# One core, a hybrid encoder block: token sums of x from a second copy, Strassen sums over twelve rounds, and matmuls of ones at the start

## The chip, the core and the metric

The kernel runs on one core of a Trainium2 chip. Its time is the device time of one execution in microseconds (us). A profile of one execution shows what each engine did: TensorE (PE, with its weight loads PEld), VectorE (DVE), ScalarE (ACT), GpSimd (POOL) and SyncE (SP), which issues most loads. Each engine works through its own instructions in a fixed order and waits for others by semaphores.

## The reference, cut to what matters

The block takes x (512 tokens of 2048 features, float32). Its first part is a normalisation by token and a product with a wide weight:

```python
def rms_norm(x, g):
    y = x32 * lax.rsqrt(jnp.mean(x32 * x32, axis=-1, keepdims=True) + EPS)
    return (y * g).astype(x.dtype)
a = rms_norm(h, attn_norm_g[i])
z = a @ w_in[i]          # q, k, v, and the two halves of a gated MLP
```

After it come differential attention with a relative-position bias, a spatial gate, an output product, a SwiGLU network, a gated per-layer input and a last normalisation. The change touches only the first normalisation and the first products.

## The kernel before, in words

All arrays are float32. A large product is made of three matmuls with a split operand: the high half is a cast to float32r (ScalarE, line 132, `whi`, or with a scale line 136), the low half is the value less that cast (VectorE, line 133, `wlo`, or line 137). A product is high by high, high by low and low by high. Each matmul is 128 by 128 by 512 columns.

x lies features by tokens (`xT`): 16 tiles of 128 features by 512 tokens. `load_x` (line 470) loads a tile on SyncE's queue and splits it, scaled by the norm's gain of the feature. The factor 1/rms of the token is applied to the products later.

The first stage (lines 507 to 554) makes three blocks of z. Blocks 0 and 1 are made together in eight rounds: a round loads four weight slabs of 128 by 256 (`load_w4`, line 510; in the first round as four loads and two splits, later as two loads and one split), loads x tiles two rounds' worth ahead, and does 24 matmuls (line 524, `products`). Block 2 follows in four rounds of the same size, 24 matmuls each; so there are 288 matmuls. Their results are stored by GpSimd's queue (line 530).

Beside its matmuls each of the eight rounds makes the Strassen sums of one pair of x tiles (`sums`, line 480): two scaled copies on ScalarE (lines 485, 486), four scaled sums on VectorE (line 493), and a split of the four (lines 132, 133). They are the stationary operand `op4` of the next stage, the stream over `w_vg` (`stream`, line 208, matmuls on line 316), which makes seven products instead of eight. `sums` also squares both x tiles on ScalarE (lines 425, 429) and GpSimd adds the squares (line 430). Early in the stream four small matmuls by ones (line 439) turn the added squares into sums by token, and `rsqrt` (line 445) makes the factors `rt`, which the stream's results need (line 570).

The order on each engine is laid down when the kernel is built, by a scheduler that takes instructions by priority as soon as their inputs are expected; `tc.high_priority` puts loads and splits of weights and of x ahead. On-chip memory is handed out in pools from the left and the right; when a pool is closed, tiles of a later pool may lie where its tiles lay, and then wait for their last use. The first stage's pools p0, p1, p2 lie at the right; the stream's w7x (four raw tiles, six halves) and b7x (four tiles `b12`, four `t1`) are opened at the left after those are closed.

Of the kernel before, what the change touches and what calls it, by code (L numbers as in the profile page):

```python
# [11 lines left out]
F32 = mybir.dt.float32  # L12
F32R = mybir.dt.float32r
AF = mybir.ActivationFunctionType
# [5 lines left out]
P = 128  # L20
D = 2048
T = 512
KT = D // P
# [8 lines left out]
CK = 4  # L32
# [3 lines left out]
RAWS = 4  # L36
PRIO = 80
FIRST = 4
XB = 12
KP = KT // 2  # L40
TAB = 3 * P
BIAS_W = 5 * P
# [31 lines left out]


@with_exitstack
def block_kernel(ctx: ExitStack, tc: tile.TileContext, out, xT, pT, w_in, w_vg, w_out, w13, w2,
                 w_up, w_gate, gains, fgain, subg, lam_v, rel_bias, onehot, lng, lnb, wsT, bsp):
    nc = tc.nc
    const = ctx.enter_context(tc.tile_pool(name="const", bufs=1))  # L80
    sm = ctx.enter_context(tc.tile_pool(name="sm", bufs=4))
    dr = ctx.enter_context(tc.tile_pool(name="dr", bufs=1, space=DRAM))
    pt = ctx.enter_context(tc.tile_pool(name="pt", bufs=2, space=PSUM))

# [4 lines left out]
    ident = const.tile([P, P], F32, name="ident")  # L89
    make_identity(nc, ident)  # L90
    ones = const.tile([P, P], F32, name="ones")
    nc.vector.memset(ones, 1.0)
    mhalf = const.tile([P, 4], F32, name="mhalf")
    nc.vector.memset(mhalf, -0.5)
    gain = const.tile([P, 2, KT], F32, name="gain")
    nc.scalar.dma_start(out=gain, in_=gains)
    ngain = const.tile([P, KT], F32, name="ngain")
    nc.vector.tensor_scalar(out=ngain, in0=gain[:, 0], scalar1=-1.0, scalar2=None, op0=ALU.mult)

# [345 lines left out]
    def rsqrt(ss, n, count, r=None):  # L445
        v = sm.tile([P, 4], F32, name="v")
        nc.vector.tensor_scalar(out=v[:, :n], in0=ss, scalar1=1.0 / count, scalar2=EPS,
                                op0=ALU.mult, op1=ALU.add)
        if r is None:
            r = sm.tile([P, 4], F32, name="r")  # L450
        nc.gpsimd.tensor_tensor(r[:, :n], v[:, :n], mhalf[:, :n], op=ALU.pow)  # L451
        return r
# [4 lines left out]
    ca = cap.__enter__()  # L457


    xop, xs, rt = [], [], []  # L460
    zqk = dr.tile([3, P, 2, T], F32, name="zqk")
    zg = dr.tile([2, 2, P, 2, T], F32, name="zg")
    with pool("osm", bufs=1) as osm:
        pcp, pap, pbp = (pool(n, side="right", bufs=1) for n in ("p0", "p1", "p2"))
        pc, pa, pb = pcp.__enter__(), pap.__enter__(), pbp.__enter__()
        pp = ctx.enter_context(ppp := ExitStack()).enter_context(
            pool("ppx", bufs=1, space=PSUM))
        rms = Rms(D, pc.tile([P, T], F32, name="acc"))

        def load_x(n):  # L470
            for k in range(len(xop), min(n, KT)):
                xt = pb.tile([P, T], F32, name="xt", bufs=XB)
                o = op_tile(opa)
                with tc.high_priority(PRIO):
                    nc.sync.dma_start(out=xt, in_=xT[:, k])
                    split((o[:, 0], o[:, 1]), xt, gain[:, 0, k:k + 1])
                xop.append(o)
                xs.append(xt)

        def sums(c):  # L480
            (g0, g1), n0 = (gain[:, 0, 2 * c + e:2 * c + e + 1] for e in range(2)), \
                ngain[:, 2 * c:2 * c + 1]
            x11, x21, x12, x22 = (xs[2 * c + e][:, n:n + 256] for e in range(2) for n in (0, 256))
            a = pa.tile([P, 2, 256], F32, name="a2")
            nc.scalar.activation(a[:, 0], x22, AF.Copy, scale=g1)
            nc.scalar.activation(a[:, 1], x11, AF.Copy, scale=g0)
            for e in range(2):
                rms.add(xs[2 * c + e], pa)
            t = pa.tile([P, 4, 256], F32, name="t4")
            for o, x, y, v, f in ((0, x21, a[:, 0], g0, ALU.add), (1, x11, t[:, 0], n0, ALU.add),  # L490
                                  (2, x12, t[:, 1], g1, ALU.subtract),
                                  (3, x21, a[:, 1], n0, ALU.add)):
                nc.vector.scalar_tensor_tensor(out=t[:, o], in0=x, scalar=v, in1=y, op0=ALU.mult,
                                               op1=f)
            o = osm.tile([P, 4, 2, 256], F32R, name="op4", bufs=KP)
            split((o[:, :, 0], o[:, :, 1]), t)
            return o

        def stationary(c, o):
            def at(i, x, s):  # L500
                if 0 < i < 5:
                    return o[:, i - 1, x, s * P:(s + 1) * P]
                n = s + (2 if i == 6 else 0)
                return xop[2 * c + (i > 0)][:, x, n * P:(n + 1) * P]
            return at

        load_x(1)
        ps = [pp.tile([P, 2, T], F32, name="c", bufs=3) for _ in range(3)]

        def load_w4(src):  # L510
            raw = pb.tile([P, CK, 256], F32, name="raw", bufs=3)
            hi = pa.tile([P, CK, 256], F32R, name="whi", bufs=2)
            lo = pa.tile([P, CK, 256], F32R, name="wlo", bufs=2)
            with tc.high_priority(PRIO):
                for u, v in src:
                    for i, w in u:
                        nc.sync.dma_start(out=raw[:, i], in_=w)
                    split((hi[:, v], lo[:, v]), raw[:, v])
            return hi, lo

        def products(ps, hi, lo, n, k):
            for m in range(2):
                for i, (a, b) in enumerate(((hi, 0), (hi, 1), (lo, 0))):
                    nc.tensor.matmul(ps[:, m], lhsT=a[:, n, m * P:(m + 1) * P], rhs=xop[k][:, b],  # L524
                                     start=k == 0 and i == 0, stop=k == KT - 1 and i == 2)

        def store(j, n):
            t = ca.tile([P, 2, T], F32, name=n)
            nc.vector.tensor_copy(t, ps[j])
            nc.gpsimd.dma_start(out=zqk[j], in_=t)  # L530

        sop = []
        for c in range(KP):
            u = [[(slice(2 * j + n, 2 * j + n + 1) if c == 0 else slice(2 * j, 2 * j + 2),
                   w_in[4 * j, :, 2 * c + n:2 * c + n + (1 if c == 0 else 2)]) for j in range(2)]
                 for n in range(2 if c == 0 else 1)]
            hi, lo = load_w4([(u[n], slice(n, 4, 2)) for n in range(2)] if c == 0
                             else [(u[0], slice(0, 4))])
            load_x(2 * c + 3)
            for k in range(2):  # L540
                for j in range(2):
                    products(ps[j], hi, lo, 2 * j + k, 2 * c + k)
            sop.append(stationary(c, sums(c)))
        for k0 in range(0, KT, CK):
            hi, lo = load_w4([([(slice(0, CK), w_in[1, :, k0:k0 + CK])], slice(0, CK))])
            if k0 == 0:
                store(0, "c21")
                store(1, "c12")
            for j in range(CK):
                products(ps[2], hi, lo, j, k0 + j)  # L550
        store(2, "c21")
        pbp.__exit__(None, None, None)
        pap.__exit__(None, None, None)
        pcp.__exit__(None, None, None)


        cbp = pool("cb", side="right", bufs=1)
        cb = cbp.__enter__()
        z = {}

        def result(g, n):
            z[n] = (ca if n in ("c12", "c21") else cb).tile([P, 2, T], F32, name=n)
            return z[n]

        def finish_z(g, n, t, later, s=None, acc=None):
            u, f = int(n[1]) - 1, int(n[2]) - 1
            for s in range(2):
                nc.scalar.activation(t[:, s], (t if acc is None else acc)[:, s],
                                     AF.Copy if g else AF.Gelu_apprx_tanh,
                                     scale=rt[0][:, 2 * u + s:2 * u + s + 1])  # L570
            if not g:
                nc.gpsimd.dma_start(out=zg[u, f], in_=t)

        with pool("w7x", bufs=1) as w7, pool("b7x", bufs=1) as b7:
            stream(w7, w7, b7, b7, pp, [Phase(
                w_vg, [(g, 0, KP // 2) for g in range(2)], lambda g, k: sop[k],
                combine(result, finish_z), at={2: [(lambda: rt.append(rms.token()), ())]})])
        ppp.close()
    rt = rt[0]
    wpp = pool("wpa", bufs=2)  # L580
    rp = wp = wpp.__enter__()
    pscp = pool("psc", bufs=1, space=PSUM)
# [37 lines left out]
    def prelude():  # L620
        diag = hp.tile([P, 4, P], F32, name="diag", tag="aT")
        for t in range(4):
            nc.vector.tensor_scalar(out=diag[:, t], in0=ident, scalar1=rt[:, t:t + 1],
                                    scalar2=None, op0=ALU.mult)
        ps = pt.tile([P, T], F32, name="pt")
        nc.tensor.matmul(ps, lhsT=ones, rhs=diag.rearrange("p t q -> p (t q)"), start=True,
# [189 lines left out]
    sop = []  # L816
# [394 lines left out]
```

## Time and profile before

| | us |
|---|---|
| median of 3 runs | 2188.73 |
| lowest, highest run | 2186.42, 2191.08 |
| profiled execution, its own time | 2185.85 |
| span from its first to its last instruction | 2183.7 |
| TensorE busy | 2130.8 (98%) |
| VectorE busy | 1640.0 (75%) |
| ScalarE busy | 1026.9 (47%) |
| GpSimd busy | 249.1 (11%) |

The mean granted clock of TensorE is 0.994 of 2.4 GHz. Times in rows count from the span's start. A matmul's time in a row is from its start to its modelled end, and matmuls overlap; how far starts lie apart tells their pace.

### The profile page before, as it was taken

Reading aid. Unit: us, or ns where it says so; the run is one execution under the profiler, and the core shown is the slowest. Engines: PE = TensorE matmul, PEld = TensorE weight load, DVE = VectorE, ACT = ScalarE, POOL = GpSimd, SP = SyncE. Lnnn points to the kernel's source line nnn. Section 1 sums busy time; section 2 is a strip of 40 time slices with the busy share of each in tenths; the row PEclk is TensorE's granted clock in tenths of the full one; section 3 lists DMA queues with packets and bytes.
Section 4 is the critical chain, followed back from the end, with each engine's and each line's share of the span. In section 5 each row is a group of like instructions: output and inputs, shape, how many; then the busy total and the mean of one; then the engine's idle time right before and its main releaser. Section 6 shows DMA issues by size and latency. Waiting matters only on the chain. (4 is left out here: it accounts for less than half of the span.)

```text
span 2183.7 us, 25457 instructions
## 1 busy us (share of the span) xinstructions
PE 2130.8 (98%) x9514; PEld 1745.2 (80%) x9514; DVE 1640.0 (75%) x1762; ACT 1026.9 (47%) x1295; POOL 249.1 (11%) x378
## 2 busy tenths in 40 slices
PE   7999999999999899999999999999999999999997
PEld 5788777878887688888888888888778888888885
DVE  8677565455535787798788788778788877789896
ACT  6354323355434454554555455455443333346555
POOL 4000300001221000000000000003312202100000
PEclk9999999999999999999999999999999999999999
DMA  5443532223445435534544553557967837536535
GB/s 174 164 147 105 180 108 68 87 78 108 143 138 185 120 121 159 191 121 141 183 151 128 176 173 129 160 186 219 317 230 224 269 116 233 179 111 215 192 105 179
DMA packets 112346, 350.24 MB, mean 160 GB/s; under 512 B 12976, under 2 KB 14512, under 8 KB 112224
## 3 DMA queue, kind: packets, MB, share of 16 engines
q1 hardware_dynamic: 67904, 233.86, 34.6%
q0 software_dynamic: 41056, 107.16, 14.4%
q10 hardware_dynamic: 3264, 7.62, 0.9%
q8 instruction: 74, 1.21, 0.2%
q14 instruction: 48, 0.39, 0.1%
HBM read 286.46 MB, written 62.13 MB: 160 GB/s over the span
## 5 line engine op out<-in xcount | busy, mean ns | idle before, releaser
L316 PE MATMUL c<-whi,op 128*128 128x512 f32 x4592 | 1422.6, 391 | 8.7 <-ACT op L198 5.7
L316 PEld LDWEIGHTS c<-whi,op 128*128 128x128 f32 x4592 | 858.2, 188 | 188.4 <-ACT op L198 6.4
L316 PE MATMUL c<-wlo,op 128*128 128x512 f32 x2296 | 895.6, 390 | 7.2 <-DVE wlo L133 7.1
L132 ACT CAST whi<-raw 128x1024 fp32r<-128x1024 f32 (+1 forms) x331 | 347.0, 1050 | 489.7 <-PE c L316 290.8
L133 DVE TENSOR_TENSOR wlo<-raw,whi 128x1024 fp32r<-128x1024 f32 (+1 forms) x331 | 403.3, 1221 | 216.8 <-ACT whi L132 211.9
L316 PEld LDWEIGHTS c<-wlo,op 128*128 128x128 f32 x2296 | 431.3, 188 | 101.5 <-DVE wlo L133 11.2
L132 ACT CAST whi<-t 128x1024 fp32r<-128x1024 f32 x246 | 259.1, 1053 | 314.1 <-PE c L316 283.9
L168 PE MATMUL ps<-op,whi 128*128 128x512 f32 x1088 | 349.1, 400 | 0.0
L133 DVE TENSOR_TENSOR wlo<-t,whi 128x1024 fp32r<-128x1024 f32 x246 | 299.8, 1220 | 34.0 <-ACT whi L132 32.3
L239 DVE TENSOR_TENSOR t<-raw,t 128x1024 f32<-128x1024 f32 x164 | 200.5, 1222 | 78.4 <-DMA raw<-w 64.7
L168 PEld LDWEIGHTS ps<-op,whi 128*128 128x128 f32 x1088 | 201.3, 188 | 44.4 <-issue 3.6
L168 PE MATMUL ps<-op,wlo 128*128 128x512 f32 x544 | 213.4, 392 | 0.0
L395 POOL DMA_DIRECT2D gs<-o x88 | 47.3, 538 | 768.0 <-DVE o L133 718.1
L132 ACT CAST whi<-b 128x1024 fp32r<-128x1024 f32 x82 | 86.4, 1054 | 87.7 <-PE c L316 87.7
L133 DVE TENSOR_TENSOR wlo<-b,whi 128x1024 fp32r<-128x1024 f32 x82 | 100.1, 1221 | 33.1 <-ACT whi L132 32.8
L168 PEld LDWEIGHTS ps<-op,wlo 128*128 128x128 f32 x544 | 102.1, 188 | 21.6
L239 DVE TENSOR_TENSOR b<-raw,b 128x1024 f32<-128x1024 f32 x82 | 100.1, 1221 | 20.1 <-DMA raw<-w 18.0
L939 POOL DMA_DIRECT2D op<-gs x154 | 83.1, 540 | 253.2 <-PE c L316 238.9
L239 DVE TENSOR_TENSOR t<-b,raw 128x1024 f32<-128x1024 f32 x82 | 101.3, 1236 | 5.7 <-DMA b<-w_vg 2.3
L340 DVE TENSOR_TENSOR c<-c,c 128x1024 f32<-128x1024 f32 x63 | 76.9, 1221 | 14.0 <-PE c L316 14.0
L132 ACT CAST o<-t 128x512 fp32r<-128x512 f32 x88 | 49.1, 569 | 76.3 <-DMA gs<-o 48.1
L524 PE MATMUL c<-op,whi 128*128 128x512 f32 x192 | 61.9, 404 | 9.0 <-ACT whi L132 9.0
(173 smaller groups left out, 1230.8 us busy)
## 6 DMA issues: line engine op xcount, KB each, us to landing
raw<-w SPq DMA_DIRECT2D x198, 512.0 KB, 3.8
op<-gs POOLq DMA_DIRECT2D x154, 256.0 KB, 4.7
b<-w SPq DMA_DIRECT2D x66, 512.0 KB, 4.4
gs<-o POOLq DMA_DIRECT2D x66, 512.0 KB, 3.3
raw<-w_in SPq DMA_DIRECT2D x40, 512.0 KB, 3.6
raw<-w_out SPq DMA_DIRECT2D x32, 512.0 KB, 3.6
raw<-w_vg SPq DMA_DIRECT2D x24, 512.0 KB, 3.6
raw<-w_gate SPq DMA_DIRECT2D x24, 512.0 KB, 4.2
```

Source lines behind the costliest of these rows:

```text
L132: recent[:] = (nc.scalar.copy(out=hi, in_=src), nc.vector.tensor_tensor(out=lo, in0=src, in1=hi.bitcast(F32), op=ALU.subtract))
L133: nc.vector.tensor_tensor(out=lo, in0=src, in1=hi.bitcast(F32), op=ALU.subtract))
L168: nc.tensor.matmul(ps[:, m], lhsT=a[:, j, ms], rhs=op[k][:, b], start=k == 0 and i == 0, stop=k == nk - 1 and i == 2)
L239: nc.vector.tensor_tensor(o, x, y, op=ALU.subtract)
L316: product[:] = [nc.tensor.matmul(p, lhsT=f.op(g, k)(i, x, s), rhs=y[:, e], start=k == 0 and i in (0, 1, 5) and (x, y) == (0, whi), stop=k ...
L340: (eng or nc.vector).tensor_tensor(o, x, y, op=ALU.add)
L395: nc.gpsimd.dma_start(out=gs[j, :, n:n + m], in_=o[:, :m].bitcast(F32))
L524: nc.tensor.matmul(ps[:, m], lhsT=a[:, n, m * P:(m + 1) * P], rhs=xop[k][:, b], start=k == 0 and i == 0, stop=k == KT - 1 and i == 2)
L939: nc.gpsimd.dma_start(out=sop[p + e][:, i], in_=gs[k + e, :, i])
```

## The change

A second copy of x by tokens (`xn`, four blocks of 128 tokens by 2048) becomes an input. Four times, GpSimd's queue loads a block into one tile and ScalarE squares it and adds each row up in the same instruction; `rsqrt` on the four columns gives `rx`, which takes the place of `rt`. The squares by feature, GpSimd's additions and the four matmuls by ones in the stream go. The Strassen sums are made in rounds 2 to 5 and 7 to 10 of the twelve, the squares in rounds 1, 3, 5 and 7. x has sixteen tiles instead of twelve. The first round's weights are split in four quarters, each behind its own load. A small copy on ScalarE and ten 128x128 matmuls of ones by ones come right after the constants. A tile of 64 bytes is put in the left-hand memory.

```diff
-XB = 12
+    ctx.enter_context(tc.tile_pool(name="padl", bufs=1)).tile([P, 16], F32, name="padl")
     nc.scalar.dma_start(out=gain, in_=gains)
+    nc.scalar.copy(out=const.tile([P, 4], F32, name="first"), in_=mhalf)
+    ps = pt.tile([P, T], F32, name="pt")
+    for _ in range(10):
+        nc.tensor.matmul(ps[:, :P], lhsT=ones, rhs=ones, start=True, stop=True)
...
-        rms = Rms(D, pc.tile([P, T], F32, name="acc"))
+        ssx = pc.tile([P, 4], F32, name="ssx")
+        def squares_x(t):
+            x = pc.tile([P, D], F32, name="xn", bufs=1)
+            nc.gpsimd.dma_start(out=x, in_=xn[t])
+            nc.scalar.activation(x, x, AF.Square, accum_out=ssx[:, t:t + 1])
...
-                xt = pb.tile([P, T], F32, name="xt", bufs=XB)
+                xt = pb.tile([P, T], F32, name="xt", bufs=KT)
...
-            for e in range(2):
-                rms.add(xs[2 * c + e], pa)
...
+        def step(n):
+            for c in {2: (0,), 3: (1,), 4: (2,), 5: (3,), 7: (4,), 8: (5,), 9: (6,), 10: (7,)}.get(n, ()):
+                sop.append(stationary(c, sums(c)))
+            if n in (1, 3, 5, 7):
+                squares_x(n // 2)
         for c in range(KP):
-            hi, lo = load_w4([(u[n], slice(n, 4, 2)) for n in range(2)] if c == 0
-                             else [(u[0], slice(0, 4))])
+            if c == 0:
+                hi, lo = load_w4([([(slice(2 * j + n, 2 * j + n + 1), w_in[4 * j, :, n:n + 1])],
+                                   slice(2 * j + n, 2 * j + n + 1)) for n in range(2)
+                                  for j in range(2)])
+            else:
+                hi, lo = load_w4([([(slice(2 * j, 2 * j + 2), w_in[4 * j, :, 2 * c:2 * c + 2])
+                                    for j in range(2)], slice(0, 4))])
...
-            sop.append(stationary(c, sums(c)))
+            step(c)
         for k0 in range(0, KT, CK):
...
+            step(KP + k0 // CK)
+        rx = const.tile([P, 4], F32, name="rx")
+        rsqrt(ssx, 4, D, rx)
...
-                combine(result, finish_z), at={2: [(lambda: rt.append(rms.token()), ())]})])
+                combine(result, finish_z))])
```

## Rows read from the trace of the kernel before

**Rows 1.** Busy time by stretch: stretch, length, engines, granted clock, DMA share, GB/s.

```profile
8.23:68.00 59.77, 52.46 (x207) 40.35 (x208) 57.31 (x65) 39.86 (x63) 23.83 (x16) 0.97 0.45 146
10.00:15.00 5.00, 5.00 (x19) 3.94 (x18) 5.00 (x8) 5.00 (x9) 2.05 (x1) 1.00 1.02 370
43.38:46.44 3.06, 3.06 (x7) 2.44 (x8) 3.03 (x3) 1.30 (x3) 2.68 (x2) 0.52 0.56 170
```

**Rows 2.** TensorE's waits, 0 to 250 us: total, times, longest.

```profile
PE c L524 <- ACT whi L132: 9.0, 2, 8.2
PE c L524 <- DVE wlo L133: 6.6, 5, 3.3
PE c L316 <- ACT whi L132: 0.7, 2, 0.5
```

**Rows 3.** Instructions grouped, 0 to 87 us: busy, mean ns, idle before.

```profile
L430 POOL TENSOR_TENSOR acc<-acc,sq 128x512 f32<-128x512 f32 x15 | 23.5, 1566 | 28.7 <-ACT sq L429 28.1
...
L137 DVE SCALAR_TENSOR_TENSOR op<-xt,gain,op 128x512 fp32r<-128x512 f32 x16 | 15.7, 1003 | 0.8 <-ACT op L136 0.8
...
L132 ACT CAST whi<-raw 128x1024 fp32r<-128x1024 f32 x13 | 13.4, 1044 | 5.9 <-PE c L524 5.7 <-ACT whi L132 0.2
...
L429 ACT ACTIVATE sq<-xt 128x512 f32<-128x512 f32 x15 | 8.9, 621 | 2.5 <-POOL acc L430 2.5
...
L493 DVE SCALAR_TENSOR_TENSOR t<-xt,gain,a 128x256 f32<-128x256 f32 x8 | 7.8, 969 | 0.1
L493 DVE SCALAR_TENSOR_TENSOR t<-xt,ngain,a 128x256 f32<-128x256 f32 x8 | 6.9, 864 | 0.0
L493 DVE SCALAR_TENSOR_TENSOR t<-xt,gain,t 128x256 f32<-128x256 f32 x8 | 5.7, 713 | 0.2
L493 DVE SCALAR_TENSOR_TENSOR t<-xt,ngain,t 128x256 f32<-128x256 f32 x8 | 4.8, 606 | 0.0
```

**Rows 4.** Lines 493 and 137 by themselves: ns shortest, median, longest.

```profile
L493 DVE SCALAR_TENSOR_TENSOR t<-xt,gain,a x8: 476/936/1527, 9.6 to 65.0; 128x256 f32<-128x256 f32 x8
...
L137 DVE SCALAR_TENSOR_TENSOR op<-xt,gain,op x16: 740/746/1780, 5.9 to 41.4; 128x512 fp32r<-128x512 f32 x16
```

**Rows 5.** TensorE in order of time: start, duration, instruction.

```profile
8.23 1.22 PE L524 MATMUL c<-op,whi 128*128 128x512 f32 x2 [8.23 <-ACT whi L132]
...
12.24 0.63 PE L524 MATMUL c<-op,whi 128*128 128x512 f32 x2
...
77.70 0.61 PE L524 MATMUL c<-op,whi 128*128 128x512 f32 x2
...
86.54 0.61 PE L316 MATMUL c<-whi,op 128*128 128x512 f32 x2
...
96.42 0.95 PE L439 MATMUL pt<-ones,acc 128*128 128x1 f32 x8
97.23 0.49 PE L316 MATMUL c<-wlo,op 128*128 128x512 f32 x1
```

**Rows 6.** All engines in order of time, the first 8 us.

```profile
0.83 0.17 DVE L92 MEMSET ones<- 128x128 f32 x1 [0.83 <-PEq L1201]
...
1.28 0.72 POOL L612 DMA_DIRECT2D sg<-subg  x1 [0.34 <-issue]
...
3.81 1.28 ACT L136 ACT_TABLE_LOAD   x1 [3.81 <-DMA xt<-xT]
...
7.58 1.12 ACT L132 CAST whi<-raw 128x512 fp32r<-128x512 f32 x2
```

**Rows 7.** TensorE's instructions grouped, whole span: busy, mean ns, idle before.

```profile
L758 PE MATMUL pt<-wb,z 128*128 128x128 f32 x64 | 8.6, 278 | 0.3 <-DVE mixed L762 0.3
```

**Rows 8.** SyncE's queue in order of time, about the turn to the stream.

```profile
65.44 1.95 SPq L229 DMA_DIRECT2D raw<-w_vg  x4
86.50 1.75 SPq L229 DMA_DIRECT2D b<-w_vg  x4
```

**Rows 9.** DMA issues, 0 to 260 us: KB each, median us to landing.

```profile
zqk<-c POOLq DMA_DIRECT2D x3, 512.0 KB, 8.3
```

More of the change, by code (lines that the diff above doesn't have):

```diff
@@ L76, in block_kernel @@
 @with_exitstack
-def block_kernel(ctx: ExitStack, tc: tile.TileContext, out, xT, pT, w_in, w_vg, w_out, w13, w2,
+def block_kernel(ctx: ExitStack, tc: tile.TileContext, out, xT, xn, pT, w_in, w_vg, w_out, w13, w2,
                  w_up, w_gate, gains, fgain, subg, lam_v, rel_bias, onehot, lng, lnb, wsT, bsp):
@@ L457, in block_kernel @@
     ca = cap.__enter__()
-    xop, xs, rt = [], [], []
+    xop, xs = [], []
     zqk = dr.tile([3, P, 2, T], F32, name="zqk")
@@ L532, in block_kernel @@
         sop = []
-        for c in range(KP):
-            u = [[(slice(2 * j + n, 2 * j + n + 1) if c == 0 else slice(2 * j, 2 * j + 2),
-                   w_in[4 * j, :, 2 * c + n:2 * c + n + (1 if c == 0 else 2)]) for j in range(2)]
-                 for n in range(2 if c == 0 else 1)]
-            hi, lo = load_w4([(u[n], slice(n, 4, 2)) for n in range(2)] if c == 0
-                             else [(u[0], slice(0, 4))])
+        def step(n):
[3 more added lines that the diff above has]
+                squares_x(n // 2)
+        for c in range(KP):
+            if c == 0:
[5 more added lines that the diff above has]
+                                    for j in range(2)], slice(0, 4))])
             load_x(2 * c + 3)
@@ L569, in finish_z @@
                                      AF.Copy if g else AF.Gelu_apprx_tanh,
-                                     scale=rt[0][:, 2 * u + s:2 * u + s + 1])
+                                     scale=rx[:, 2 * u + s:2 * u + s + 1])
             if not g:
@@ L576, in block_kernel @@
                 w_vg, [(g, 0, KP // 2) for g in range(2)], lambda g, k: sop[k],
-                combine(result, finish_z), at={2: [(lambda: rt.append(rms.token()), ())]})])
+                combine(result, finish_z))])
         ppp.close()
-    rt = rt[0]
     wpp = pool("wpa", bufs=2)
@@ L622, in prelude @@
         for t in range(4):
-            nc.vector.tensor_scalar(out=diag[:, t], in0=ident, scalar1=rt[:, t:t + 1],
+            nc.vector.tensor_scalar(out=diag[:, t], in0=ident, scalar1=rx[:, t:t + 1],
                                     scalar2=None, op0=ALU.mult)
@@ L1178 @@
         "xT": _tokens(a["x"][0]),
+        "xn": np.ascontiguousarray(a["x"][0].reshape(T // P, P, D)),
         "pT": _tokens(a["p"][0, 0]),
```

## The prediction

> **What bounds the kernel now.** TensorE is busy for 98% of the span, so only stretches in which it waits or runs at half rate can give time back. I read the table of stretches first, then TensorE's waits in the first 250 us, then the instructions of those stretches. From 8.23 to 68 us VectorE is busy for 57.3 of 59.8 us, more than TensorE (52.5), and GpSimd works for 23.8 us beside it [rows 1]. TensorE's waits there end with the two weight splits, ScalarE's high half and VectorE's low half: 9.0 us in two waits, of which 8.2 are the start, and 6.6 us in five [rows 2]. After that, up to 250 us, there is 0.7 us of waiting. So the place of the change is the only stage of the first 250 us with much to give.
>
> Why VectorE is late is in the grouped instructions. The 32 Strassen sums of x (L493) have means of 969, 864, 713 and 606 ns, the 16 low halves of x (L137) 1003 ns [rows 3]; but the shortest of a sum is 476 ns, the median of L137 746 ns, and the longest 1527 and 1780 ns [rows 4]. The long ones lie beside GpSimd's 15 additions of squares (L430, 1566 ns each). Without that neighbour the sums would take 32 x 0.476 = 15.2 us instead of 25.2, the low halves 11.9 instead of 15.7 (their minima and medians): 13.8 us of VectorE's 57 are lost to GpSimd.
>
> **How much lies in the stage.** Its matmuls start at 8.23 and the stream's first starts at 86.54, 78.31 us for 288 matmuls. Where nothing waits, 39 of them start between 77.70 and 86.54: 0.2267 us each [rows 5], so the 288 need 65.3 us and 13.0 us are lost after the start. Of these the first nine take 4.01 us (8.23 to 12.24) instead of 2.04: 2.0 us at half rate. After the wait of 3.3 us seven more take 3.06 us instead of 1.59, with a granted clock of 0.52, the 1.2 GHz level [rows 1]: 1.5 us. Waits after the start are 7.4 us; the rest, 2.1 us, is the tail of matmuls drawn longer than their spacing, and lies with the waits.
>
> **The change part by part.**
>
> *Token sums from a copy by tokens.* Sixteen squares of 128x512 on ScalarE (621 ns) and fifteen additions on GpSimd go. Four squares of 128x2048 come: by the squares' 621 ns for 512 columns and the cast's 1044 ns for 1024 [rows 3], 0.83 ns a column, so an estimate of 1.9 us each, 7.6 for 9.9 before. GpSimd's neighbour work and the 13.8 us go. The four small matmuls by ones at 96.42 go too: the next product starts at 97.23, so 0.8 us [rows 5].
>
> *Sums over twelve rounds.* A round has 24 matmuls, 5.44 us. VectorE's work in one, undisturbed: two low halves of x 1.49, the low half of the weights 1.22, four sums 1.9, their low half 1.22, in all 5.8 us by durations (somewhat less, since starts follow closer than durations); without sums 2.7. Before, all eight rounds have sums: 46 us against TensorE's 43.5, and 60 with GpSimd. Now five of the first eight do: 8 x 2.7 + 5 x 3.1 = 37 us. The other three go into rounds with one weight split, 1.22 + 3.1 = 4.3 us. VectorE is no longer the bound in any long run of rounds. ScalarE in rounds 3, 5 and 7 has two high halves of x (1.4), a cast of weights and one of sums (1.04 each), two scalings (1.0) and a square (1.9): 6.4 us, over 5.44, but 2.4 to 4.5 in the rounds between. So the 11.0 us of waits and lowered clock inside the stage should nearly all go; bounds 0 and 11.0.
>
> *Start.* Before, ScalarE begins its table load when x lands, at 3.81, and then splits three x tiles ahead of the weights' cast at 7.58 [rows 6]. Now a copy of a small tile takes the 1.28 us load before the data, and the first cast needs a quarter of the tile. The first split from 3.81 takes 0.7, a 128x256 operation of ScalarE 0.5: the earliest matmul is at 5.0, the latest at 8.2 as now. I take 5.6, since later loads share the queue: 2.6 us. Four quarter operations for two half ones cost two more starts on ScalarE, and on VectorE: 0.4 us, which I charge.
>
> *Matmuls of ones.* A matmul of 128x128 in float32 shows as two records: 64 for the 32 calls of L758, 8.6 us, 0.134 us each at the upper clock [rows 7]. Ten calls are 2.7 us at 2.4 GHz, 5.4 at 1.2. They can start when the ones are written, 1.00 [rows 6], and end between 3.7 and 6.4, so they hold the first product up by 0.8 us at most. Before, the rate rises after 4.0 us of work [rows 5]; about as much work now lies ahead of the first product. I credit the 2.0 us; bounds 0 and 2.0.
>
> *New cost: 4.2 MB of x again.* GpSimd has no work before the first of these loads; that it issues early what stands far down in the program is seen in L612's load at 1.28 [rows 6]. So the first 1.05 MB comes with the first weights. From 10 to 15 us the engines of the DMA are full, share 1.02 at 370 GB/s [rows 1]; at that rate 1.05 MB are 2.8 us. The first rounds need 1.05 MB each in 5.44 us, 193 GB/s, and the copy 96 GB/s more if it keeps two rounds apart: 289, under 370. So a delay at the start, none later: bounds 0 and 2.8, taken 2.0. By the Trainium skill's page "DMA: Bandwidth & Descriptors", section "Issuing engines are not separate DMA queues", loads from GpSimd and from SyncE run on the same 16 engines, so the second queue gives nothing but issue time; by it the sum would carry the full 2.8 for 2.0. No run of before has both queues loaded in this stage.
>
> *New wait.* Each square waits in ScalarE's queue for its load, and behind it stand casts of weights, for which TensorE waits. The next load waits for the square before, since there is one buffer. A round or two of distance covers it; for a first one placed early I charge 1.5 us, and 0.5 for rounds 3, 5 and 7. Bound 0 below; above, see the last rival.
>
> *Nothing.* The rsqrt on four values lies beside products. Sixteen x tiles instead of twelve take away a wait of the load queue. On GpSimd's queue the loads L612 and L614 and the three stores of products now stand behind loads of the copy; the first two are used after the stream, and the stores come after the last square's load.
>
> **The sum.** Off: 2.6 + 2.0 + 11.0 + 0.8 = 16.4 us. On: 0.4 + 2.0 + 1.5 + 0.5 = 4.4. Net 12.0 us. After the stage TensorE hardly waits, so the gain stays. The profiled execution took 2185.85 us (span 2183.7 and 2.15 around), the median of the timed ones 2188.73, 2.9 more. 12.0 off give 2173.9 against the first and 2176.7 against the median, which I predict.
>
> **The rivals.**
>
> *The start is starved.* If the copy is loaded as fast as its buffer comes free, 4.2 MB compete with the first five rounds, not one. At 370 GB/s that is 11.3 us of transfer; slack is 370 - 193 = 177 GB/s, so over the 27 us of five rounds 4.8 MB fit, and the loss is uneven delivery, say 4 to 6 us more: 2181.5. For: the share of 1.02. Against: the waits of TensorE end with splits, none with a load [rows 2]. Chance 0.15. The rule of the skill's page named above points this way.
>
> *The turn to the stream.* Twelve x tiles become sixteen and an 8 KB tile comes, while 2 KB of sums and two 2 KB squares go: the right-hand pools grow by 10 KB. The stream's first four raw tiles, which now load at 65.44 without a wait, may come to lie on them; its other four already wait for the last product, to 86.50 [rows 8]. If all wait, TensorE stands still for landing and split, some 5 us, and 1.5 at the lower clock: 2183.2. Against: x tiles are free when their sums are done, a round before the end. Chance 0.10.
>
> *ScalarE takes VectorE's place.* It has 6.4 us in every second round, and its small waits meet VectorE's. Then only start, clock and the four small matmuls remain, 5.4, less 4.4: 2187.7, within the 0.2% (4.4 us) that a measurement can tell. Against: 39.9 us of ScalarE in 59.8 [rows 1]. Chance 0.08.
>
> *Slower: squares hold ScalarE up.* If the order written out for ScalarE puts each square right behind the load's expected landing and the load is later than expected, all casts wait. ScalarE's own work in the first eight rounds is about 32 us (39.9 less three sums' share and some of the squares). With four waits of w, the stage ends at 5.6 + 32 + 4w + 21.8 (four rounds); that passes 86.54 at w = 6.8 us. Transfers of half that size from GpSimd's queue took 8.3 us from issue to landing [rows 9]. With w = 8.3 it ends at 92.6, later by 6.1, less 0.8: 2194.0. Against: in the program the squares stand two rounds, 10.9 us, apart. Chance 0.06.
>
> **How the numbers follow.** The forecast has the remaining 0.61, with its own range of 2172 to 2180. Low end: all 16.4 off and the lowest run, 2.3 under the median, 2170. High end: the first two rivals with an execution's spread, 2185; beyond it lie the last two cases. Faster by over 0.2% are the forecast, nearly all of the first two rivals: 0.84; within 0.2% 0.10; slower 0.06.
>
> **What would show it.** Right: ten matmuls of ones from about 1 us; the first product at 5 to 6.5, at full spacing; L493 near 0.48 us throughout; VectorE's share before 68 us well under its 96%; no granted clock below 1.00 in the stage; the stream's first product at 73 to 76. Wrong: TensorE waiting for ScalarE's casts behind L429's successor, a wait of the load queue at the turn, first products beyond 8 us, or a stage that ends early while the span does not shrink.

## The result, and the profile after

The changed kernel takes 2205.81 us (median of 5 runs, 2204.07 to 2208.5), the kernel before beside it 2187.07 (5 runs, 2185.71 to 2191.08): a ratio of 1.009, 95% interval 1.0079 to 1.0102. The forecast was 2176.7 us. The profiled execution took 2204.07 us with a span of 2202.0, 18.3 more than before.

One row splits that. The stream's first product comes at 80.76 us (86.54 before, [rows 5]), so 5.8 us are won up to there; from it to the end it is 2121.2 us for 2097.2, so 24.0 are lost in a stretch that the diff hardly touches.

TensorE of the changed kernel in order of time (start, duration, instruction, in brackets the wait before it):

```profile
1.05 3.93 PE L100 MATMUL pt<-ones 128*128 128x128 f32 x20 [1.05 <-DVE mhalf L94]
4.97 0.99 PE L531 MATMUL c<-op,whi 128*128 128x512 f32 x2
...
12.04 2.07 PE L531 MATMUL c<-op,whi 128*128 128x512 f32 x4 [5.04 <-ACT whi L136]
...
17.32 0.82 PE L531 MATMUL c<-op,whi 128*128 128x512 f32 x2
...
77.95 0.64 PE L531 MATMUL c<-op,whi 128*128 128x512 f32 x2
...
80.76 0.63 PE L320 MATMUL c<-whi,op 128*128 128x512 f32 x2
```

The first product starts at 4.97 instead of 8.23. Then TensorE stands still for 5.04 us, and runs at half rate after that: the 12 matmuls between 12.04 and 17.32 take 5.28 us, where 12 x 0.2267 are 2.72. At the end of the stage nothing waits, and still the 12 matmuls between 77.95 and 80.76 take 2.81 us, 0.234 each. In [rows 5] 39 of them took 8.84, 0.227 each.

The same kernel by stretches (stretch, length, busy time of PE, PEld, DVE, ACT, POOL with counts, granted clock, DMA share, GB/s):

```profile
2.00:10.00 8.00, 5.00 (x24) 3.83 (x22) 1.66 (x4) 2.14 (x6) 0.31 (x1) 1.00 0.90 291
...
8.23:68.00 59.77, 55.96 (x228) 44.87 (x229) 47.78 (x71) 42.22 (x59) 4.93 (x8) 0.94 0.72 247
...
12.00:14.00 2.00, 1.96 (x5) 1.58 (x6) 1.96 (x5) 2.00 (x2) 0.00 (x0) 0.50 0.93 323
14.00:16.00 2.00, 2.00 (x6) 1.55 (x5) 1.39 (x4) 2.00 (x6) 1.50 (x3) 0.50 1.09 368
...
700.00:1500.00 800.00, 793.06 (x3500) 644.91 (x3499) 647.24 (x664) 402.03 (x465) 42.25 (x76) 1.00 0.47 149
```

and the last stretch in the kernel before:

```profile
700.00:1500.00 800.00, 792.35 (x3560) 654.03 (x3559) 656.98 (x675) 407.61 (x470) 45.43 (x82) 1.00 0.48 154
```

VectorE has 47.78 us of work in the stage for 57.31 [rows 1]. The granted clock is 0.50, the 1.2 GHz level, behind the wait. In the 800 us far behind the stage TensorE is as busy as before at a granted clock of 1.00, and has done 60 matmuls fewer: 1.7%. So no wait and no clock explains the loss; each matmul takes longer.

VectorE and ScalarE of the changed kernel, grouped, 0 to 82 us (busy, mean ns, idle before):

```profile
L500 DVE SCALAR_TENSOR_TENSOR t<-xt,gain,t 128x256 f32<-128x256 f32 x8 | 3.9, 484 | 0.2
L500 DVE SCALAR_TENSOR_TENSOR t<-xt,gain,a 128x256 f32<-128x256 f32 x8 | 3.9, 481 | 0.3
...
L477 ACT ACTIVATE xn<-xn 128x2048 f32<-128x2048 f32 x4 | 7.6, 1908 | 1.5 <-DMA xn<-xn 1.5
```

The Strassen sums take 0.48 us each, as forecast, and the squares 1.91 each. TensorE's waits of over 0.15 us, 0 to 100 us (total, times, longest); the last line is of the stream:

```profile
PE c L531 <- ACT whi L136: 5.0, 1, 5.0
PE pt L100 <- DVE mhalf L94: 1.1, 1, 1.1
PE c L320 <- ACT whi L136: 0.7, 2, 0.5
```

So in the stage it waits for nothing after 12.04.

### The profile page after: what moved, and what is told of

It reads as the page before. It is cut to its first block, busy times and chain, and to the rows that moved or that the text cites. A ratio compares the mean times of both kernels' runs of the same rounds, so it can differ in the third digit from the quotient of the medians.

```text
span 2202.0 us, 25455 instructions
## 1 busy us (share of the span) xinstructions
PE 2161.0 (98%) x9526; PEld 1752.6 (80%) x9526; DVE 1628.9 (74%) x1764; ACT 1027.0 (47%) x1290; POOL 226.6 (10%) x367
## 4 chain that ended last, share of the span: by engine, by line
PE 91%; DMA 3%; DVE 3%; issue 2%; ACT 1%; POOL 0%; SPq 0%; DVEq 0%; POOLq 0%; ACTq 0%
PE c L320 67%; PE ps L172 16%; PE c L531 3%; DMA raw<-w 2%; DVE wlo L137 1%; PE c L302 1%; PE pt L384 1%; PE sc L709 1%; PE pt L740 1%; DVE t L243 0%; DMA xt<-xT 0%; ACT whi L136 0%; PE pt L776 0%; PE pt L844 0%; DMA bias<-dtab 0%
## 5 line engine op out<-in xcount | busy, mean ns | idle before, releaser
L320 PE MATMUL c<-whi,op 128*128 128x512 f32 x4592 | 1439.9, 395 | 8.5 <-ACT op L202 5.7
L320 PE MATMUL c<-wlo,op 128*128 128x512 f32 x2296 | 905.0, 394 | 4.8 <-DVE wlo L137 4.7
```

The lines of the kernel that those rows point to most:

```text
L320: product[:] = [nc.tensor.matmul(p, lhsT=f.op(g, k)(i, x, s), rhs=y[:, e], start=k == 0 and i in (0, 1, 5) and (x, y) == (0, whi), stop=k ...
```

## The experiments

Ratios are against the kernel before on the same chip (its medians there: 2185.73, 2185.47, 2185.83 and 2185.38), with 95% intervals. "Tail" is the time from the stream's first product to the end of the span in the profiled execution. It is one execution of each kernel, and those of one kernel can lie 10 us apart (e4: 2177.15 to 2187.44), so a tail that is some us longer is a sign, and the medians and intervals decide.

| run | median us | ratio | stream's first | tail |
|---|---|---|---|---|
| before | 2185.38 to 2187.07 | 1 | 86.54 | 2097.2 |
| changed | 2205.81 | 1.009 [1.0079, 1.0102] | 80.76 | 2121.2 |
| e3: before, left +128 bytes | 2208.91 | 1.0103 [1.0088, 1.0118] | 86.92 | 2122.6 |
| e8: before, both sides +128 | 2185.91 | 0.9999 [0.999, 1.0009] | 86.98 | 2097.1 |
| e11: before, left +64 | 2194.4 | 1.0042 [1.0027, 1.0058] | 87.28 | 2102.7 |
| e1: changed, left as before | 2187.06 | 1.0005 [0.9996, 1.0015] | 80.46 | 2105.5 |
| e2: e1, right as before too | 2185.2 | 1.0001 [0.9991, 1.0011] | 80.55 | 2102.0 |
| e4: e2, first copy held | 2183.92 | 0.9991 [0.9979, 1.0002] | 80.08 | 2101.1 |
| e5: e4, four ones | 2177.79 | 0.9966 [0.9954, 0.9978] | 78.20 | 2096.9 |
| e6: before, six ones | 2191.4 | 1.0021 [1.0012, 1.003] | 86.26 | 2105.5 |
| e12: before, 64 ones | 2204.87 | 1.0091 [1.0076, 1.0106] | 104.85 | 2097.0 |
| e13: before, 70 ones | 2212.84 | 1.0128 [1.0111, 1.0145] | 107.61 | 2102.3 |
| e7: e5, copy from round 4 | 2174.4 | 0.9946 [0.9933, 0.996] | 74.63 | 2096.9 |
| e10: e7, sums in eight rounds | 2174.66 | 0.9945 [0.9932, 0.9957] | 74.98 | 2097.7 |

**Theories.** First theory: the diff's small tiles shift whole memory regions, and a matmul's pace depends on how the addresses of its two operands stand to each other. By the addresses that the compiler gave, all split operands of the kernel before start at 128 past a multiple of 256 bytes. In the changed kernel those in the left-hand memory start at a multiple of 256, those at the right still at 128 past, the stage's weights at 96. The left side has moved by 128 bytes: 64 of the tile in the diff, 32 that ScalarE's small copy takes, and 32 because `rx` and the later `rt` no longer share one place. Rivals: the new order of the instructions makes the long stretch slower, or the loads of the copy do.

**e1, e3: the left side alone.** e1 puts the left-hand tiles of the changed kernel back to 128; e3 moves those of the kernel before, and changes nothing else.

```diff
# e1, from the changed kernel
-tile_pool(name="padl", bufs=1)).tile([P, 16], F32, name="padl")
+tile_pool(name="padl", bufs=1)).tile([P, 48], F32, name="padl")
# e3, from the kernel before
+ctx.enter_context(tc.tile_pool(name="padl", bufs=1)).tile([P, 32], F32, name="padl")
```

> The changed kernel with the left-hand pad tile at 192 bytes a partition instead of 64, so that the left-hand tiles lie a further 128 bytes up and are again congruent modulo 256 bytes with the right-hand ones. Theory (the pace of a matmul depends on whether its moving and its stationary operand start at the same address modulo 256 bytes): the 6216 matmuls of the later streams go back from 231 to 227 ns, some 27 us less, about 2179 us against 2187 of the kernel before (0.996); the first stage stays at 234 ns. Rival (the 18.7 us are waits or contention of the new order, and the pad is without effect): 2206, 1.009.

> The kernel before with nothing but a left-hand pad tile of 128 bytes a partition. Theory: its first stage and its later streams fall to 231 to 234 ns where the operands now differ by 128 modulo 256, the stream over w_vg and the products of w_in and w_out stay at 227; about 28 us more, 2215 (1.013). Rival (the loss is of the new order): as before, 2187, 1.000.

e1 wins 18.7 us of the 27 expected over the changed kernel, and an unused tile of 128 bytes alone makes the kernel before as slow as the changed one. The 800 us of e3, then of e1, by the same columns as above:

```profile
700.00:1500.00 800.00, 792.85 (x3494) 644.57 (x3493) 648.01 (x664) 400.97 (x462) 46.36 (x75) 0.99 0.48 150
```

```profile
700.00:1500.00 800.00, 788.73 (x3535) 649.13 (x3534) 651.30 (x672) 405.92 (x468) 45.10 (x81) 1.00 0.48 152
```

e3 has 66 matmuls fewer than the kernel before without any of the change's instructions; that is against both rivals. e1 gets 35 of the changed kernel's 60 back, not all.

**e8, e11: is it the address or the difference?** e8 shifts both sides by 128 bytes; e11 the left by 64.

```diff
# e8, from the kernel before
+ctx.enter_context(tc.tile_pool(name="padl", bufs=1)).tile([P, 32], F32, name="padl")
-tile_pool(name="pad", side="right", bufs=1)).tile([P, 24], F32, name="pad")
+tile_pool(name="pad", side="right", bufs=1)).tile([P, 56], F32, name="pad")
# e11, from the kernel before
+ctx.enter_context(tc.tile_pool(name="padl", bufs=1)).tile([P, 16], F32, name="padl")
```

> The kernel before with both pads 128 bytes larger, so that all tiles of both sides lie 128 bytes further in and are congruent with each other again. Theory (only the difference of the operands' addresses modulo 256 bytes counts): pace 227 ns and time as before, 2186 (1.000). Rival (each operand's own address counts): slower as with the left pad alone, 2209 (1.010).

> The kernel before with nothing but a left-hand pad tile of 64 bytes a partition, so that the operands of the first stage and of five eighths of the later streams differ by 64 bytes modulo 256. Theory: slow as with 128 bytes, 231 to 234 ns for a matmul, 2205 to 2212 us (1.010). Rival (only a difference of 128 counts, or the grain is 64 bytes): as before, 2186 (1.000).

With both sides shifted the time is that of before; so it is the difference that counts. 64 bytes cost 8.6 us, 128 cost 23: neither expectation for e11 had a step in between. Every matmul of the first stage, the streams and the products with w_in and w_out, matched with its operands' addresses, gives the start-to-start pace (of those under 300 ns whose next matmul has the same pair of addresses; the last two rows are of the first stage, the others of the streams):

| addresses modulo 256 bytes, moving and stationary operand | matmuls | mean ns | median ns |
|---|---|---|---|
| 0 and 0 (e8) | 6720 | 227.1 | 227 |
| 192 and 192 (e11) | 2548 | 227.5 | 227 |
| 192 and 128 (e11) | 3592 | 229.3 | 229 |
| 0 and 128 (e3) | 3594 | 232.7 | 232 |
| 0 and 0 (e3) | 2534 | 228.1 | 227 |
| 128 and 96 (e1, first stage) | 271 | 233.5 | 234 |
| 0 and 96 (changed, first stage) | 270 | 234.3 | 234 |

3594 x (232.7 - 227.1) = 20.1 us of e3's 23, and 3592 x (229.3 - 227.1) = 7.9 of e11's 8.6. In the kernel before the two addresses differ by 0, 256, 512 or 768 bytes modulo 1024, 2053 to 2199 matmuls of each, and the median is 227 ns for all four; so 256 is the grain. The loss does not grow with the distance: 32 apart (e1's first stage) costs as much as 96 or 128, 64 apart less than half. Why the hardware does this was not settled.

**e2: the right side too.** A tile of 56 floats beside the small tile of squares' sums puts the stage's weights back to 128 past.

```diff
         ssx = pc.tile([P, 4], F32, name="ssx")
+        pc.tile([P, 56], F32, name="padr")
```

> As the run before, and a 224-byte pad tile beside the tile of row sums on the right, so that the first stage's weights are congruent too. Theory: the first stage's 288 matmuls also go from 234 to 227 ns, 2 us more, about 2177 us (0.995). Rival (address without effect): 2206, 1.009.

Addresses now stand as before, yet e2 is level with the kernel before, not 2177. The stage's matmuls are back at 227 ns, but it still ends at 80.55: the first product comes 0.3 us later than in e1, at 5.34, and there are two waits for low halves, 1.0 us, that the changed kernel does not have. The tail is 2102.0, 4.8 longer than before. So the stage and the tail each hide another loss.

**e4: the copy's first load.** Its tile is first written by a small copy that needs the last quarter of the first weights, so the load can't start before them.

```diff
             x = pc.tile([P, D], F32, name="xn", bufs=1)
+            if t == 0:
+                nc.vector.tensor_copy(x[:, 0:1], last[0][:, 3, 0:1].bitcast(F32))
```

> The second run's kernel, with the first load of the copy by tokens held until VectorE has made the low half of the last quarter of the first weights (one extra 128x1 copy on VectorE). Theory (the first load of the copy takes half of the DMA engines from the first x tiles and weights, so that TensorE waits 5.0 us at 7 us and then runs at half rate): that wait falls under 1 us, the half rate does not come back, the stream's first product starts 5 to 7 us sooner, about 2171 us (0.992 to 0.993). Rival (the wait is for ScalarE's order, not for data): as the second run, 2177, and the wait stays.

All engines of the changed kernel in order of time show why (GpSimd's load of the copy, ScalarE's split of the second x tile):

```profile
1.29 0.70 POOL L476 DMA_DIRECT2D xn<-xn  x1 [0.36 <-issue]
...
9.95 0.72 ACT L140 ACTIVATE op<-xt,gain 128x512 fp32r<-128x512 f32 x1 [4.62 <-DMA xt<-xT]
```

TensorE of e2, then of e4, in order of time:

```profile
11.79 2.12 PE L532 MATMUL c<-op,whi 128*128 128x512 f32 x4 [3.97 <-ACT whi L136]
```

```profile
8.27 1.20 PE L534 MATMUL c<-op,whi 128*128 128x512 f32 x4 [1.22 <-ACT whi L136]
```

The wait, 5.04 us in the changed kernel and 3.97 in e2, is 1.22, and these four matmuls take 1.20 us where they took 2.07 and 2.12: no half rate. But the stage ends only 0.5 earlier than e2's. ScalarE's waits for the copy in e4, 0 to 85 us, and TensorE's in the stage (total, times, longest):

```profile
ACT xn L480 <- DMA xn<-xn: 6.7, 3, 3.4
```

```profile
PE c L534 <- ACT whi L136: 3.5, 4, 1.2
PE c L534 <- DVE wlo L137: 1.8, 4, 0.7
```

The last of the squares that waits, and what stands behind it (all engines of e4 in order of time):

```profile
46.23 1.92 ACT L480 ACTIVATE xn<-xn 128x2048 f32<-128x2048 f32 x1 [2.09 <-DMA xn<-xn]
...
49.08 1.04 ACT L136 CAST whi<-raw 128x1024 fp32r<-128x1024 f32 x1
...
50.17 0.73 PE L534 MATMUL c<-op,whi 128*128 128x512 f32 x2 [0.96 <-ACT whi L136]
...
51.62 0.77 PE L534 MATMUL c<-op,wlo 128*128 128x512 f32 x1 [0.72 <-DVE wlo L137]
```

The squares now wait for their loads, and the casts of weights behind them. Of TensorE's 5.3 us of waits (3.5 + 1.8) 2.1 lie before 15 us, ahead of the first square (19.22), and 3.2 behind squares. Behind the two at 50 to 52 us the lower clock is back, in the same columns as the stretches above:

```profile
52.00:54.00 2.00, 2.00 (x6) 1.52 (x6) 1.24 (x3) 1.60 (x3) 0.00 (x0) 0.50 0.67 172
```

So most of what the start won was given back by squares that stand in rounds 1 to 7.

**e5, e6: the number of TensorE's instructions.** The tail of e4 is still 4 us too long, in an order of instructions that is the same as before from 250 us on. A matmul in float32 is two records, and each comes with a weight load, so ten ones are 40 instructions for the 16 of the four token matmuls: 24 more. Theory: TensorE's code is loaded in pieces of 16384 bytes (75 of them, queue q8, some 128 matmuls and as many weight loads apart), and 24 instructions more shift each piece by 12 matmuls against the loads of weights that it meets. Rival: the matmuls of ones or more instructions cost time in themselves.

```diff
# e5, from e4
-    for _ in range(10):
-        nc.tensor.matmul(ps[:, :P], lhsT=ones, rhs=ones, start=True, stop=True)
+    for _ in range(4):
+        nc.tensor.matmul(ps[:, :320], lhsT=ones, rhs=ones[:, 0:1].broadcast_to([P, 320]), ...)
# e6, from the kernel before
+    for _ in range(6):
+        nc.tensor.matmul(ps[:, :P], lhsT=ones, rhs=ones, start=True, stop=True)
```

> The fourth run's kernel with four matmuls of ones of 320 columns in place of ten of 128: the same columns in all, but 16 records on TensorE instead of 40, as many as the four matmuls by ones that the stream no longer has, so that TensorE's instructions in the later streams stand at the same count as before the change. Theory (24 more instructions shift the fetches of TensorE's code some 12 matmuls earlier, into loads of weights that are then 1 to 2 us late, so that TensorE waits for VectorE's low halves in the stream over the FFN's first weights): those waits go, the first group of 900 matmuls of that stream takes 218 us instead of 220, and the whole about 5 us less than the fourth run, 2179 us against 2186 (0.997). Rival (the waits come from the new input's place in memory or from the shifted tiles): as the fourth run, 2184.

> The kernel before with nothing but six matmuls of ones of 128 columns at its start: 24 more records on TensorE, as the change has in sum. Theory (place of the code fetches): the first products save some 1 to 2 us of half rate, and the later streams lose 4 to 6, about 2189 us (1.001 to 1.002). Rival (place of the fetches without effect): 2184 (0.999).

Four wider ones, 16 instructions, bring the tail to 2096.9, and 6.1 us in all (1.9 of them in the stage). Six ones in the kernel before cost 0.21%, 4.6 us, though its stage ends no later; its profiled execution, 2193.97, lies 2.6 above its median, so its tail in the table is too long by as much. The trace of e2 shows the place (VectorE and TensorE in order of time):

```profile
828.04 1.23 DVE L243 TENSOR_TENSOR t<-raw,t 128x1024 f32<-128x1024 f32 x1 [1.36 <-DMA raw<-w]
...
830.45 0.50 PE L320 MATMUL c<-wlo,op 128*128 128x512 f32 x1 [0.70 <-DVE wlo L137]
```

A raw tile lands late, VectorE's sum of it waits, and 2.4 us later TensorE waits for a low half. VectorE's waits between 740 and 1500 us (total, times, longest), e2 and e5:

```profile
DVE t L243 <- DMA raw<-w: 51.7, 38, 3.0
```

```profile
DVE t L243 <- DMA raw<-w: 31.2, 35, 2.0
```

The kernel before has 36.9 in 37. In e5 and before TensorE waits for nothing in that stretch, in e2 three times, 1.4 us; those waits are only a part of the loss, for from 765 to 1485 us (matmuls 2900 to 6000) e2's starts fall 3.3 us behind those of the kernel before. The losses stand at fixed places. With the matmuls of 512 columns counted from 0, the starts that come over 150 ns late, and do not in the kernel before, are number 3188, number 3200 or a multiple of 336 behind one of these, and twice 3164. There are three to eight of them in each of e1, e2, e4, e6 and e13, the kernels with the streams at 227 ns and the code shifted by 24. Of those without the shift e5, e10 and e12 have none, e7 and e8 one each.

**e12, e13: a whole piece of code more.** This tells the place of the code from the number of instructions.

```diff
# from the kernel before; 70 for 64 in e13
+    ps = pt.tile([P, T], F32, name="pt")
+    for _ in range(64):
+        nc.tensor.matmul(ps[:, :1], lhsT=ones, rhs=ones[:, 0:1], start=True, stop=True)
```

> The kernel before with 64 matmuls of ones (128x128 by one column, 128 matmul records and as many weight loads) at the start. If what six matmuls of ones cost the kernel before (ratio 1.0021) comes from the place of the code loads, 256 instructions more are one whole load of 16384 bytes at 64 bytes each, so every load of code stands beside the same matmuls as in the kernel before: from the stream's first product to the end it takes 2097.2 us as before (within 1.5), VectorE waits 37 us for raw tiles between 740 and 1500 us, TensorE not at all. The time as a whole grows only by what the start is later, 0 to 6 us. If instead more instructions on TensorE, or matmuls of ones at the start as such, cost time, that stretch is longer by at least the 4.5 us of the six.

> The same with 70 one-column matmuls of ones, 24 instructions past the whole load. By the place of the code loads, it stands as with six: the stretch from the stream's first product to the end is 4 to 5 us longer than with 64, VectorE's waits for raw tiles between 740 and 1500 us rise to about 51 us, and the time is 4 to 5 us above that with 64, of which the six themselves are at most 1.2. By the rivals it is within 1.2 us of the kernel with 64.

The start was mis-sized: the 128 one-column matmul records take 27.5 us, and the stream begins 18.3 us later, not 0 to 6; with six more 2.8 later again, not 1.2. The tail decides. With 256 instructions more it is 2097.0, with 280 it is 2102.3. Leaving out the one piece more that the ones of e12 and e13 fill, the first pieces of code come at matmul 82, 215, 330, 456 in e12, and at 80, 216, 329, 456 in the kernel before; in e13 at 79, 207, 328, 439, and in e6 at 71, 201, 328, 438 (matmuls of 512 columns that had started). VectorE's waits in the same stretch, e12 and e13:

```profile
DVE t L242 <- DMA raw<-w: 39.7, 38, 2.5
```

```profile
DVE t L242 <- DMA raw<-w: 52.2, 37, 2.8
```

The rival falls: the larger number of instructions is free in the tail when it is a whole piece.

**e7, e10: the copy later, and the sums back.** e7 moves the squares to rounds 6, 8, 9 and 11 and the first load behind round 4's weights; e10 is e7 with the Strassen sums in the first eight rounds again.

```diff
# e7, from e5
-                nc.vector.tensor_copy(x[:, 0:1], last[0][:, 3, 0:1].bitcast(F32))
+                nc.vector.tensor_copy(x[:, 0:1], last[4][:, 3, 0:1].bitcast(F32))
-            if n in (1, 3, 5, 7):
-                squares_x(n // 2)
+            if n in (6, 8, 9, 11):
+                squares_x((6, 8, 9, 11).index(n))
# e10, from e7
-            for c in {2: (0,), 3: (1,), 4: (2,), 5: (3,), 7: (4,), 8: (5,), 9: (6,), 10: (7,)}.get(n, ()):
+            for c in ({n: (n,) for n in range(8)}).get(n, ()):
```

> The run with four matmuls of ones, with the squares in rounds 6, 8, 9 and 11, where ScalarE has fewer splits, and the first load of the copy held until round 4. Theory: ScalarE neither waits for the copy nor holds casts up, the first stage takes 68 to 70 us from its first product instead of 75, and the whole is 5 to 7 us under the run before it, about 2173 us (0.994). Rival (the first stage is held up by its own x and weights, not by the copy): 2179, and its waits stay.

> The run with late squares, with the sums back in the first eight rounds. Theory (what freed VectorE is that GpSimd no longer works beside it; with sums in each round VectorE still has 5.3 to 5.8 us of work in a round of 5.44): the first stage is 1 to 3 us longer than the 69.5 us of that run, about 2176 us. Rival (the spread over twelve rounds is what frees VectorE): VectorE is late again as in the kernel before, the stage takes 75 us or more, 2180.

e7 beats both kernels: 11.1 us under the kernel before (2185.47 beside it), 31.4 under the changed one. Its TensorE in order of time:

```profile
1.05 4.63 PE L100 MATMUL pt<-ones 128*128 128x320 f32 x8 [1.05 <-DVE mhalf L94]
5.13 1.50 PE L534 MATMUL c<-op,whi 128*128 128x512 f32 x2
...
13.92 1.20 PE L534 MATMUL c<-op,whi 128*128 128x512 f32 x4 [1.62 <-ACT whi L136]
...
74.63 0.62 PE L320 MATMUL c<-whi,op 128*128 128x512 f32 x2
```

Two waits are left in the stage, 1.62 and 0.25 us, both before 16 us, and the stream begins at 74.63. ScalarE still waits 7.1 us for the copy, against what was expected, but in rounds where TensorE does not feel it. e10 is the same within its interval, so spreading the sums over twelve rounds is worth nothing that these runs can tell once GpSimd no longer adds beside them.

## Why the prediction was wrong, point by point

**Right: what holds VectorE up in the stage.** GpSimd gone, the sums take 0.48 us and the waits behind VectorE (6.6 us in [rows 2]) vanish. The changed kernel's stage ends at 80.76 all the same, for the reasons below. In e7, with start, layout, ones and squares changed, the stream begins at 74.63; the prediction's terms without the four token matmuls give 86.54 - 15.6 + 4.4 = 75.3. e7's gain of 11.1 us stands against the 12.0 forecast. That the sums meet so closely is in part luck: the forecast's 4.0 us behind the first product are for the copy (2.0 + 2.0), while e7 loses 4.2 (69.5 less 65.3), nearly all of it before 16 us, where no square stands.

**Wrong: "After the stage TensorE hardly waits, so the gain stays".** This step failed, with 24.0 us. Its first half held (in the 800 us TensorE is busy for 793.06 as against 792.35); the gain went because every matmul of some streams is slower. The prediction took the 0.2267 us of [rows 5] for a property of the matmul; it is one of two operands that lie alike. The places that the diff's 64-byte tile, the small tiles of the copy and of the factors, and the one for the squares' sums take were put at nothing without a reason: the prediction prices none of these places. Taking their shift back is worth some 20 us (2205.81 to 2185.2 from the changed kernel to e2), and the shift of the left side alone, in e3, lengthens the tail by 25.4 us (23 in the medians), as much as the change does. A second loss, of 4 to 5 us, shows once the pace is back (e2, e4) and goes with the number of ones (e5): their price was worked out as time at the start, 0 to 0.8, and that 24 instructions shift all code behind them was not thought of. So the two do not simply add up: between 740 and 1500 us the changed kernel itself, at its slower pace, has no wait of TensorE. What the ten ones cost there was not run by itself.

**Mis-sized: the copy at the start.** Forecast 2.0 us of delay, bounds 0 and 2.8. Measured: 5.04 us of waiting, and 2.6 us at half rate behind it (5.28 - 2.72), so the 2.0 credited to the ones came back and more. The bound divided bytes by a full rate; it did not see that the second x tile, needed next, stands among them: ScalarE waits 4.62 us for it. This is the rival "the start is starved", with its 4 to 6 us, but by the first load alone. By the Trainium skill's page "DMA: Bandwidth & Descriptors", section "Issuing engines are not separate DMA queues", loads from two queues interleave on the same engines; the trace agrees: with both at work the second x tile came at 9.95 us, at a DMA share of 0.90 from 2 to 10 us.

**Mis-placed: sums over twelve rounds.** The prediction counted VectorE's work down from 46 to 37 us by the spread. e10 shows that eight rounds do as well once GpSimd no longer takes its 13.8 us.

**Too cheap: the squares' waits.** Charged 2.0 us in all. In e4, with the start mended, ScalarE waits 6.7 us for the copy, TensorE 3.2 behind squares, and the lower clock comes on top. With the squares from round 6 on (e7) TensorE has 1.8 us of waits in the whole stage, none of them behind a square.

**The signs.** Ones from 1.05, sums at 0.48 and VectorE's 47.78 of 59.77 came as said. The first product, at 4.97, came as early as said, but not at full spacing (the first three starts lie 0.50, 0.33 and 0.34 us apart); no granted clock below 1.00 and the stream at 73 to 76 did not come. "A stage that ends early while the span does not shrink" was named as a sign of being wrong, and is what came, without a rival that had a cause for it.

## What to carry to other kernels

When a kernel is bound by matmuls, a new tile of a few bytes is a change to all of them: look at where both operands lie after the edit, and pad until they lie alike as before. When a long stretch is slower with as much busy time and the same granted clock, compare the spacing of starts before looking for waits. Hold a bulk load that is needed late behind the loads needed first, whichever queue issues it, and count added TensorE instructions, since they move the code loads of all that follows.

## What the runs showed of the hardware

A 128x512 matmul in float32r starts every 227 ns when its two operands' addresses agree modulo 256 bytes, every 229 when they are 64 apart, every 232 to 233 when 128 apart and every 234 when 32 or 96 apart, at a granted clock of 1.00; over this kernel 128 bytes are 1.0%, 64 bytes 0.4%.

Loads of TensorE's code stand among the DMA transfers of the core (queue q8, 75 pieces of 16384 bytes in the changed kernel): a shift of 24 instructions costs 0.2% of this kernel (e6), and one of 256 nothing in the tail (e12). That it is the meeting of code and weights that makes the load late was argued from the traces of e2 and the places of the pieces; no run moved a load of weights alone, so it is not shown.
